# Attention's head tiles in three pools, a third item's scores among the query products

## The chip, the cores and the metric

One core of a Trainium2 chip runs the whole kernel. The metric is device time in microseconds (us); several executions of a kernel agree within about 0.3%.

## What is computed

One transformer layer over 1024 latent tokens (a grid of 16 rows and 64 columns) and 256 context tokens, width 1024, all in fp32: a half-step SwiGLU, then two token mixers side by side on one normalised input, merged by sigmoid gates and one output projection, then a second half-step SwiGLU. The mixers are neighbourhood attention (NA) and multi-head latent attention (MLA), 8 heads each. NA, cut to what matters:

```python
rs = jnp.clip(r - kh // 2, 0, n_rows - kh)
...
bias = rpb[:, row_off[None, None, :, None], col_off[:, :, None, :]]
s_loc = jnp.einsum('bjqhd,bjakhd->bhjqak', q_r, k_b).astype(jnp.float32) + bias.astype(jnp.float32)
s_loc = jnp.where(valid[:, :, None, :], s_loc, neg).reshape(B, H, n_blk, NA_QCOLS, n_loc)
s_ctx = jnp.einsum('bjqhd,bkhd->bhjqk', q_r, k_ctx).astype(jnp.float32)
p = jax.nn.softmax(jnp.concatenate([s_loc, s_ctx], axis=-1), axis=-1).astype(v.dtype)
...
o = (jnp.einsum('bhjqak,bjakhd->bjqhd', p_loc, v_b)
     + jnp.einsum('bhjqk,bkhd->bjqhd', p[..., n_loc:], v_ctx))
```

Each latent query attends to an 8 by 16 window of the grid, with a bias by head and offset, and to all 256 context keys. MLA attends to all 1280 tokens, with keys of 64 plain and 32 rotated dimensions.

## The kernel before

Every fp32 matrix product is made of three fp32r products of high and low halves. The first SwiGLU, the projections and the second SwiGLU run from plans: lists of steps for TensorE, with side steps (loads, splits, evictions) spread over them by position (`plan.step`, `plan.spread`). The last main steps before attention are `q_heads(1)`, numbered from `o`: four rotary steps, then four products whose results are stored to scratch memory. Stores are held back some steps and written behind the last step at the latest (`store`, `flush`).

Attention follows as a loop over 64 items: 8 NA heads of 4 items (blocks of columns j, 256 queries each), then 8 MLA heads of 4. Its parts:

- An item's `scores()` makes its context and local scores in two halves (s = 0, 1); VectorE adds the bias while it evicts the local scores (L1983), copies the context scores (L1954), and ScalarE takes the exponential (L1992).
- Its `values()` has three parts for NA: `local`, `context`, `edge`. Each transposes a piece of the probabilities and returns a product with the values, which is written `LAG` = 2 parts later. So the context and edge products of item n are written inside item n + 1.
- In the loop, item n's parts are interleaved with the scores of item n + `AHEAD` (3). The first `EARLY` items' scores are made already beside the products of `q_heads(1)`, into tiles of the pool "f" (`first_scores`, `first_soft`). With EARLY = 2, item 0 of the loop makes the scores of items 2 and 3.
- `NaHead.loads` fetches a head in steps. The first fetches q, ql (high and low query), kvc (context keys, and later context values), k and the first bias table: eight transfers of 256 or 64 KB in the order q, ql, kvc, q, ql, kvc, k, k, and one bias table. The others fetch bias table 2, values va (items 0 and 1 of the head) and vb (items 2 and 3), bias table 3. For head h of 2 and more the first step is written at item 4h - 4, behind its second part (`ahead_head`), the rest at item 4h - 3, just before the first scores of head h. Item 0 of a head uses bias table 1, items 1 and 2 table 2, item 3 table 3.
- All these tiles come from the pool "w" of 13 tiles of 4 KB per partition, but for the third bias table, which comes from "y" (2 tiles). `MlaHead` takes six tiles of "w", `FirstMerge` one at a time.

A tile is given out again when its last reader in the program is through; the load into it waits for that reader. TensorE's instructions and all transfers (issued by SP, one queue) keep the order in which the program writes them; so SP runs ahead of the other engines up to the first transfer whose tile is not free, and everything behind that transfer stands. VectorE, ScalarE and GpSimd have their order in attention from the compiler's scheduler.

Of the kernel before, what the change touches and what calls it, by code (L numbers as in the profile page):

```python
# [8 lines left out]
F32 = mybir.dt.float32  # L9
F32R = mybir.dt.float32r  # L10
# [5 lines left out]
P = 128  # L16
# [22 lines left out]
def f32(ap):  # L39
    return ap.bitcast(F32)  # L40
# [3 lines left out]
def hybrid_block(ctx: ExitStack, tc: tile.TileContext, a: dict, out: bass.AP):  # L44
# [9 lines left out]
    pools = {}  # L54

    def nm(s):
        count[0] += 1
        return f"{s}_{count[0]}"

    def open_pool(key, name, bufs, side):  # L60
        pools[key] = tc.alloc_tile_pool(name=nm(name), bufs=bufs, side=side, reuse_waits="tile")

    def close_pools(*keys):
        for key in keys:
            pools.pop(key).release()

    def U(dt=F32, key="u"):
        return pools[key].tile([P, 1024], dt, tag="u", name=nm("x" + key))
# [1 line left out]
    def V(dt=F32):  # L70
        return U(dt, "v")

    def W(dt=F32R):
        return pools["w"].tile([P, 1024], dt, tag="w", name=nm("w"))

    def T2(dt=F32, n=512):
        return pools["t"].tile([P, n], dt, tag="t", name=nm("t"))
# [34 lines left out]
    class Engine:  # L112


        def __init__(self, e):
            self.e = e
# [5 lines left out]
    def ld(dst, src):  # L122
        for x in [x for x in waiting if x[1].tensor.name == src.tensor.name]:
            waiting.remove(x)
            put(*x[1:])
        return put(dst, src)
# [4 lines left out]
    def put(dst, src):  # L131
        return pin(nc.sync.dma_start(dst, src))
# [987 lines left out]
    class Raw:  # L1120

        us = {(name, hl): [U(F32R, "v") for _ in range(2)] for name in ("a11", "a12") for hl in range(2)}
        f = {}
# [95 lines left out]
    plan = Plan()  # L1219
# [23 lines left out]
    o = len(plan.main)  # L1243
# [64 lines left out]
    o = len(plan.main)  # L1308
# [12 lines left out]
    o, tail = down1.plan(plan)  # L1321
# [110 lines left out]
    def emit_lat(d, ci, x, bank):  # L1432
        t, sq = T2() if bank else x, T2()

        def high():
            if bank:
                act.copy(t, x)
            store(cqT[d][:, ci * 512:(ci + 1) * 512], t)
            act.activation(sq, t, AF.Square)
            later(add, 1)  # L1440

        def add():
            if ci in squares:
                vec.tensor_tensor(squares[ci], squares[ci], sq, op=ALU.add)
            else:
                squares[ci] = sq
        later(high)

    for p in range(3):
        punits.append(Unit(h2, [wc_cols(2 * p), wc_cols(2 * p + 1)],  # L1450
                           lambda i, ci, x, bank, p=p: emit_lat(2 * p + i, ci, x, bank)))
# [21 lines left out]
    o = len(plan.main)  # L1473
# [67 lines left out]
    class Set:  # L1541
# [16 lines left out]
        def loads(self):  # L1558

            return [lambda j=j: self.load(j) for j in range(2)]  # L1560
# [50 lines left out]
    o = len(plan.main)  # L1611
# [97 lines left out]
    class NaHead:  # L1709


        def loads(self, h):
            self.h = h
            i, b = h // 2, (h % 2) * 64
            self.q, self.ql, self.kvc, self.k = q, ql, kvc, k = [W() for _ in range(4)]
            for s in range(2):
                o = 64 * s
                ld(f32(q[o:o + 64, :]), qas[i][0, b:b + 64, :])
                ld(f32(ql[o:o + 64, :]), qas[i][1, b:b + 64, :])
                ld(f32(kvc[o:o + 64, 0:256]), kas[i][s, b:b + 64, NLAT:])  # L1720
            for s in range(2):
                ld(f32(k[64 * s:64 * s + 64, :]), kas[i][s, b:b + 64, :NLAT])
            self.bias = [W(F32)]
            ld(self.bias[0][:, :768], a["bias"][h, 0])
            yield
            self.bias.append(W(F32))
            ld(self.bias[1][:, :768], a["bias"][h, 1])
            self.va = va = W()
            for j in range(2):
                self.values(va, j)  # L1730
            yield
            ld(f32(kvc[:, 256:512]), vcs[h])
            self.vb = vb = W()
            for j in range(2, 4):
                self.values(vb, j)
            yield
            self.bias.append(U(F32, "y"))
            ld(self.bias[2][:, :768], a["bias"][h, 2])
            yield

        def values(self, v, j):
# [3 lines left out]
    def na_loads(h):  # L1745
        heads["na", h] = x = NaHead()
        yield from x.loads(h)
# [97 lines left out]
    o = va_at  # L1845
# [9 lines left out]
    o = len(plan.main)  # L1855
# [4 lines left out]
    o = len(plan.main)  # L1860
# [3 lines left out]
    o = len(plan.main)  # L1864
# [3 lines left out]
    o = len(plan.main)  # L1868
    plan.step(*calls(q_heads(1, cqn[1]), 9))
    heads = {}  # L1870
    EARLY, AHEAD = 2, 3

    na_open = {}

    def na_next(h, n=1):
        if h not in na_open:
            na_open[h] = na_loads(h)
        for _ in range(n):
            next(na_open[h], None)

    def weights():
        close_pools("v")
        open_pool("w", "weights", 13, "left")
        open_pool("f", "first", EARLY, "left")

    def score_banks():
        banks[0] = "mv"
# [3 lines left out]
    def first_scores(j):  # L1891
        if len(early) == j:
            it = na_item(0, j)
            started.append(it)
            early.append(it.scores())
        next(early[j], None)
# [3 lines left out]
            soft.pop(0)()  # L1900

    plan.spread([weights], o - 4, o - 3)
    plan.spread([lambda h=h: na_next(h) for h in (0, 0, 0, 1)], o - 3, o + 5)
    plan.spread([score_banks], o + 2, o + 3)
    plan.spread([lambda j=j: first_scores(j) for j in (0, 0, 1, 1)], o + 4, o + 8)
    plan.spread([first_soft] * 2, o + 6, o + 9)

    ona, omla = [], []

# [138 lines left out]
    class MlaHead:  # L2048
        def __init__(self, h):
            self.h = h  # L2050
            self.qh, self.ql, self.kh, self.kl, self.v, self.kvc = [W() for _ in range(6)]
            b, i = (h % 2) * 64, (h % 4) * 32
            for s, x in enumerate((self.qh, self.ql)):
                ld(f32(x[0:64, :]), qns[h // 2][s, b:b + 64, :])
                ld(f32(x[64:QK, :]), qrs[h // 4][s, i:i + 32, :])
                ld(f32(self.kvc[0:64, s * 256:(s + 1) * 256]), kns[h // 2][s, b:b + 64, NLAT:])
                ld(f32(self.kvc[64:QK, s * 256:(s + 1) * 256]), krs[s, :, NLAT:])
            for s, x in enumerate((self.kh, self.kl)):
                ld(f32(x[0:64, :]), kns[h // 2][s, b:b + 64, :NLAT])
                ld(f32(x[64:QK, :]), krs[s, :, :NLAT])  # L2060
            vsv = vs[:, h * P:(h + 1) * P].rearrange("(t p) c -> p t c", p=P)
            ld(f32(self.v).rearrange("p (t c) -> p t c", t=8), vsv[:, 0:8, :])
            ld(f32(self.kvc[:, 512:768]).rearrange("p (t c) -> p t c", t=2), vsv[:, 8:10, :])
# [70 lines left out]
    soft, started = [], []  # L2134
    edges = []
    def na_item(h, j):
        if (j == 0) if h else (j == EARLY):
            na_next(h, 4)
        return NaItem(heads["na", h], j)

# [5 lines left out]
    def items_():  # L2146
        for h in range(NH):
            for j in range(4):
                yield lambda h=h, j=j: na_item(h, j)
        for h in range(NH):  # L2150
            for b in range(4):
                yield lambda h=h, b=b: mla_item(h, b)
# [6 lines left out]

    close_pools("u", "t")  # L2160
    open_pool("o", "heads", 16, "right")
    open_pool("y", "third", 2, "right")
    open_pool("t", "half", 12, "right")
    open_pool("u", "units", 10, "right")
    for x in (ona, omla):
# [9 lines left out]
    def ahead_head(h):  # L2175
        if h < NH:
            na_next(h) if h > 1 else None
        else:
            heads["mla", h - NH] = MlaHead(h - NH)

    def start(n):

        if n < len(todo):
            it = todo[n]()
            started.append(it)
            yield from it.scores()
# [28 lines left out]
    for n in range(len(todo)):  # L2215
        ahead = chain(*[start(x) for x in (range(EARLY, AHEAD + 1) if n == 0 else (n + AHEAD,))])
        for d in range(2):
            if n == len(todo) - 6 + d:
                fm.load(d)
            if n == len(todo) - 5 + d:  # L2220
                fm.split(d)
        parts = started[n].values()
        soft_n, soft[:] = list(soft), []
        for x, part in enumerate(parts):
            pending.append(part())
            for _ in range(-(-len(soft_n) // (len(parts) - x))):
                soft_n.pop(0)()
            for _ in range(5 // len(parts)):
                next(ahead, None)
            if n % 4 == 0 and x == 2 and n // 4 + 1 < 2 * NH:  # L2230
                ahead_head(n // 4 + 1)
            if n >= len(todo) - 3 and (n, x) != (len(todo) - 3, 0) and len(fm.todo) > 4:
                fm.step()
            if len(pending) > LAG:
                pending.pop(0)()
        for _ in ahead:
            pass
    for w in pending:
        w()
        fm.step()  # L2240
# [1 line left out]
        fm.step()  # L2242
    pinned[0] = False

    close_pools("u", "t", "y", "f", "w")
    open_pool("t", "half", TBUFS, "left")
    open_pool("u", "units", 24, "left")

# [35 lines left out]
    plan = Plan()  # L2284
# [5 lines left out]
    for d in range(KD):  # L2290
        o = len(plan.main)
# [21 lines left out]
    plan = Plan()  # L2313
# [30 lines left out]
    o = len(plan.main)  # L2344
# [13 lines left out]
    o = len(plan.main)  # L2358
# [14 lines left out]
    o, tail = down2.plan(plan)  # L2373
# [108 lines left out]
```

## Time and profile before

| | us |
|---|---|
| median of 3 runs (2557.51 to 2558.33) | 2557.65 |
| profiled execution | 2555.57 |
| its span, first to last instruction | 2553.8 |
| TensorE busy in it | 2526.1 |
| VectorE busy | 1897.7 |
| ScalarE busy | 1249.9 |

The mean granted clock of TensorE is 0.999. The last query products run from 1304.7 to 1333 us of the span, NA from there to about 1457 and MLA to about 1750. In the rows that follow, PE is TensorE, PEld its weight loads, DVE VectorE, ACT ScalarE, POOL GpSimd, SP the engine that issues transfers; "SPq" is its instruction queue. `bs`, `bm`, `bv` are PSUM banks by their tag, `xf` and `xu` score tiles, `w` and `xy` tiles of the pools "w" and "y", `d` scratch memory, `t` half tiles. A timeline row gives start, length, engine, line, operation, what it writes and reads, shape, how many were merged into it, and in brackets the idle time before it with what ended it. A row of waits gives total, number and longest wait.

### The profile page before, as it was taken

Reading aid. Unit: us, or ns where it says so; the run is one execution under the profiler, and the core shown is the slowest. Engines: PE = TensorE matmul, PEld = TensorE weight load, DVE = VectorE, ACT = ScalarE, POOL = GpSimd, SP = SyncE. Lnnn points to the kernel's source line nnn. Section 1 sums busy time; section 2 is a strip of 40 time slices with the busy share of each in tenths; the row PEclk is TensorE's granted clock in tenths of the full one; section 3 lists DMA queues with packets and bytes.
Section 4 is the critical chain, followed back from the end, with each engine's and each line's share of the span. In section 5 each row is a group of like instructions: output and inputs, shape, how many; then the busy total and the mean of one; then the engine's idle time right before and its main releaser. Section 6 shows DMA issues by size and latency. Waiting matters only on the chain.

```text
span 2553.8 us, 38179 instructions
## 1 busy us (share of the span) xinstructions
PE 2526.1 (99%) x13007; PEld 2145.5 (84%) x13007; DVE 1897.7 (74%) x3627; ACT 1249.9 (49%) x2389; POOL 242.5 (9%) x425
## 2 busy tenths in 40 slices
PE   8999999999999999999999999999999999999998
PEld 6888888888888788889889999988888888888887
DVE  5788887898567687874559988886445888777557
ACT  6623223555346753333439888782355322233633
POOL 1000000000002100001007622220030000000001
PEclk9999999999999999999999999999999999999999
DMA  8477765779576665766899832215135667556755
GB/s 315 162 242 236 242 225 189 274 246 297 180 239 221 241 220 190 229 225 200 286 287 243 224 78 77 77 32 210 67 131 179 212 222 236 183 185 251 248 203 193
DMA packets 275475, 523.32 MB, mean 205 GB/s; under 512 B 33424, under 2 KB 84432, under 8 KB 275280
## 3 DMA queue, kind: packets, MB, share of 16 engines
q1 hardware_dynamic: 275280, 520.88, 61.6%
q8 instruction: 103, 1.69, 0.3%
q14 instruction: 92, 0.75, 0.1%
HBM read 375.47 MB, written 145.29 MB: 204 GB/s over the span
## 4 chain that ended last, share of the span: by engine, by line
PE 86%; ACT 6%; DVE 5%; issue 2%; POOL 0%; DMA 0%; DVEq 0%; POOLq 0%; ACTq 0%
PE bs L161 33%; PE bm L161 30%; PE bv L161 20%; ACT xu L2091 2%; PE bm L164 2%; DVE xu L1954 1%; PE bs L164 1%; ACT t L2117 1%; DVE t L2118 1%; DVE xv L120 1%; ACT xu L1992 1%; ACT t L2091 0%; ACT t L1926 0%; ACT t L120 0%; PE bv L164 0%
## 5 line engine op out<-in xcount | busy, mean ns | idle before, releaser
L120 ACT CAST xu<-t 128x512 fp32r<-128x512 f32 x589 | 346.8, 621 | 673.3 <-DVE t L120 558.1
L161 PE MATMUL bm<-xu,xu 128*128 128x512 f32 (+1 forms) x2442 | 596.0, 388 | 0.9 <-ACT t L120 0.9
L161 PEld LDWEIGHTS bm<-xu,xu 128*128 128x128 f32 x2442 | 450.1, 188 | 92.1 <-ACT t L120 2.0
L120 DVE TENSOR_TENSOR xu<-t,xu 128x512 fp32r<-128x512 f32 x589 | 383.0, 688 | 77.5 <-ACT xu L120 77.1
L161 PE MATMUL bs<-xu,xu 128*128 128x512 f32 (+2 forms) x1581 | 388.3, 384 | 0.0
L161 PE MATMUL bs<-xv,xu 128*128 128x512 f32 x1512 | 363.5, 389 | 0.2 <-DVE t L120 0.2
L161 PEld LDWEIGHTS bs<-xu,xu 128*128 128x128 f32 x1581 | 291.7, 188 | 58.0
L161 PE MATMUL bv<-xv,xu 128*128 128x512 f32 x1342 | 336.0, 389 | 0.0
L161 PEld LDWEIGHTS bs<-xv,xu 128*128 128x128 f32 x1512 | 283.5, 188 | 59.7 <-issue 1.0
L161 PEld LDWEIGHTS bv<-xv,xu 128*128 128x128 f32 x1342 | 251.6, 188 | 52.1
L120 DVE TENSOR_TENSOR xu<-xu,xu 128x512 fp32r<-128x512 f32 x282 | 190.0, 689 | 64.4 <-ACT xu L120 63.4
L120 DVE TENSOR_TENSOR t<-t,t 128x512 f32<-128x512 f32 (+4 forms) x350 | 221.2, 635 | 13.5 <-ACT t L120 8.8
L161 PE MATMUL bs<-w,w 96*128 96x512 f32 (+3 forms) x832 | 206.0, 365 | 5.4 <-DVE st L1983 5.4
L161 PE MATMUL bv<-xu,xu 128*128 128x512 f32 x722 | 191.5, 389 | 0.0
L120 POOL TENSOR_SCALAR st<-st 128x1 f32<-128x1 f32 x60 | 27.1, 452 | 1630.9 <-ACT t L120 1283.6
L120 ACT CAST xu<-xu 128x512 fp32r<-128x512 f32 x282 | 169.5, 621 | 11.3 <-DMA xu<-in_f1w 8.0
L161 PEld LDWEIGHTS bv<-xu,xu 128*128 128x128 f32 x722 | 135.5, 188 | 28.1
L161 PE MATMUL bm<-t,xu 128*128 128x256 f32 (+1 forms) x920 | 156.9, 332 | 0.0
L161 PEld LDWEIGHTS bm<-t,xu 128*128 128x128 f32 x920 | 137.4, 189 | 18.6
L161 PE MATMUL bv<-t,w 128*128 128x256 f32 x896 | 150.7, 288 | 1.9 <-DVE t L2118 1.4
L161 PEld LDWEIGHTS bv<-t,w 128*128 128x128 f32 x896 | 133.1, 190 | 17.5 <-DVE t L2118 6.0
L161 PEld LDWEIGHTS bs<-w,w 96*128 96x128 f32 (+1 forms) x832 | 123.2, 190 | 14.2 <-DVE st L1983 7.7
(231 smaller groups left out, 3192.6 us busy)
## 6 DMA issues: line engine op xcount, KB each, us to landing
d<-t SPq DMA_DIRECT2D x432, 256.0 KB, 2.9
t<-d SPq DMA_DIRECT2D x348, 256.0 KB, 5.0
xu<-in_f1w SPq DMA_DIRECT2D x104, 512.0 KB, 4.4
xu<-in_f2w SPq DMA_DIRECT2D x58, 512.0 KB, 4.7
t<-in_wada SPq DMA_DIRECT2D x112, 256.0 KB, 4.5
w<-d SPq DMA_DIRECT2D x112, 256.0 KB, 5.0
t<-in_f1w SPq DMA_DIRECT2D x77, 256.0 KB, 5.0
t<-in_f2w SPq DMA_DIRECT2D x77, 256.0 KB, 5.2
```

The source lines that it names most:

```text
L120: return lambda *x, **y: pin(f(*x, **y))
L161: return pin(nc.tensor.matmul(o, s, m, start=start, stop=stop, skip_group_check=open_group[0]))
L164: return pin(nc.tensor.transpose(o, x, i))
L1954: nc.vector.tensor_scalar(dst, src, 1.0, FMIN, op0=ALU.mult, op1=ALU.max, accum_out=m)
L1992: soft.append(lambda s=s: nc.scalar.activation(pr[s][:, :640], pr[s][:, :640], AF.Exp, bias=n_[:, s:s + 1], accum_out=l[:, s:s + 1]))
L2091: nc.scalar.activation(x, x, AF.Exp, bias=n_[:, s:s + 1], accum_out=l[:, i:i + 1])
L2117: nc.scalar.copy(t[0], pb)
L2118: nc.vector.tensor_tensor(t[1], pb, f32(t[0]), op=ALU.subtract)
```

## The change

The tiles of a head come from pools of their own kind. "w" has 8 tiles instead of 13 and holds q, ql, va, vb of every NA head, and kvc and k of the even ones; "p" (2 tiles, opened where attention opens its pools) holds kvc and k of the odd heads; "y" (4 tiles of 3 KB) all bias tables. For MLA, "w" holds query and key tiles; kvc comes from "x" (3 tiles, opened in the place of "f" when item 2 is through), the values from "p" (head 0's from "x"). EARLY is 3: three items' scores are made beside the query products, for which all four load steps of head 0 are spread there; the first step of head 1, which stood there, is now written behind the products and their stores, where attention opens its pools.

```diff
-    def W(dt=F32R):
-        return pools["w"].tile([P, 1024], dt, tag="w", name=nm("w"))
+    def W(dt=F32R, key="w", n=1024):
+        return pools[key].tile([P, n], dt, tag=key, name=nm(key))
...
-            self.q, self.ql, self.kvc, self.k = q, ql, kvc, k = [W() for _ in range(4)]
+            self.q, self.ql = q, ql = W(), W()
+            self.kvc, self.k = kvc, k = [W(key="p" if h % 2 else "w") for _ in range(2)]
...
-            self.bias = [W(F32)]
-            ld(self.bias[0][:, :768], a["bias"][h, 0])
-            yield
-            self.bias.append(W(F32))
-            ld(self.bias[1][:, :768], a["bias"][h, 1])
+            self.bias = []
+            for j in range(2):
+                self.bias.append(W(F32, "y", 768))
+                ld(self.bias[j], a["bias"][h, j])
+                if j == 0:
+                    yield
...
-            self.bias.append(U(F32, "y"))
-            ld(self.bias[2][:, :768], a["bias"][h, 2])
+            self.bias.append(W(F32, "y", 768))
+            ld(self.bias[2], a["bias"][h, 2])
...
-    EARLY, AHEAD = 2, 3
+    EARLY, AHEAD = 3, 3
...
-        open_pool("w", "weights", 13, "left")
-        open_pool("f", "first", EARLY, "left")
+        open_pool("w", "weights", 8, "left")
+        open_pool("y", "third", 4, "left")
+        open_pool("f", "first", 3, "left")
...
-    plan.spread([lambda h=h: na_next(h) for h in (0, 0, 0, 1)], o - 3, o + 5)
-    plan.spread([score_banks], o + 2, o + 3)
-    plan.spread([lambda j=j: first_scores(j) for j in (0, 0, 1, 1)], o + 4, o + 8)
-    plan.spread([first_soft] * 2, o + 6, o + 9)
+    plan.spread([lambda: na_next(0)] * 4, o - 3, o + 5)
+    plan.spread([score_banks], o + 1, o + 2)
+    plan.spread([lambda j=j: first_scores(j) for j in (0, 0, 1, 1, 2, 2)], o + 2, o + 8)
+    plan.spread([first_soft] * 3, o + 4, o + 9)
...
-            self.qh, self.ql, self.kh, self.kl, self.v, self.kvc = [W() for _ in range(6)]
+            self.qh, self.ql, self.kh, self.kl = [W() for _ in range(4)]
+            self.kvc = W(key="x")
...
+            self.v = W(key="p" if h else "x")
...
-        if (j == 0) if h else (j == EARLY):
+        if h and j == 0:
             na_next(h, 4)
...
-    open_pool("y", "third", 2, "right")
+    open_pool("p", "parts", 2, "right")
+    na_next(1)
...
+        if n == EARLY - 1:
+            close_pools("f")
+            open_pool("x", "parts", 3, "left")
```

More of the change, by code (lines that the diff above doesn't have):

```diff
@@ L2243, in hybrid_block @@
     pinned[0] = False
-    close_pools("u", "t", "y", "f", "w")
+    close_pools("u", "t", "p", "x", "y", "w")
     open_pool("t", "half", TBUFS, "left")
```

## The prediction

> **What bounds the kernel now.** I read the page first, then the stretch around the edited code by windows, then who TensorE and the DMA queue wait for there.
>
> ```profile
> PE 2526.1 (99%) x13007; PEld 2145.5 (84%) x13007; DVE 1897.7 (74%) x3627; ACT 1249.9 (49%) x2389; POOL 242.5 (9%) x425
> ```
>
> TensorE is busy 2526.1 of 2553.8 us, so a change that moves work about can win at most the 27.7 us between. What it can lose has no such limit: each idle microsecond of TensorE is added to the end. The edit touches the last query products and the neighbourhood (NA) attention:
>
> ```profile
> 1283.00:1317.00 34.00, 34.00 (x207) 30.34 (x206) 18.29 (x56) 7.44 (x14) 0.00 (x0) 1.00 1.01 309
> 1317.00:1333.00 16.00, 16.00 (x81) 13.59 (x80) 7.94 (x20) 5.90 (x10) 0.90 (x2) 1.00 0.83 245
> ```
> ```profile
> 1333.00:1343.00 10.00, 6.73 (x42) 5.35 (x41) 8.19 (x31) 6.01 (x14) 2.50 (x8) 1.00 0.78 251
> 1343.00:1460.00 117.00, 114.83 (x905) 112.17 (x904) 109.48 (x376) 108.62 (x261) 84.80 (x161) 1.00 0.91 243
> ```
>
> Columns: stretch, its length, busy time of PE, PEld, DVE, ACT, POOL, clock, DMA share, GB/s. The query products keep TensorE full with VectorE half free. The first 10 us of attention have a hole of 3.27 us. After it TensorE is full again, and the DMA engines are 91% busy: the heads' loads arrive hardly faster than they are used. TensorE's waits, from 1280 to 1460 and then from 1365 to 1460, and its two long ones:
>
> ```profile
> PE bs L161 <- DVE st L1983: 5.4, 7, 1.9
> ```
> ```profile
> PE bs L161 <- DVE st L1983: 2.1, 5, 0.7
> ```
> ```profile
> 1337.42 1.11 PE L161 MATMUL bs<-w,w 128*128 128x256 f32 x4 [1.39 <-DVE st L1983]
> ...
> 1341.92 1.10 PE L161 MATMUL bs<-w,w 128*128 128x256 f32 x4 [1.88 <-DVE st L1983]
> ```
>
> 1.39 + 1.88 = 3.27 us come from making items 2 and 3's scores at once while VectorE still drains the queries; 2.1 us in five small waits come later. That is all the change can take away here: 5.4 us, 0.21%.
>
> The DMA queue is what the edit really rearranges:
>
> ```profile
> 1289.46 5.42 SPq L132 DMA_DIRECT2D w<-d  x8
> ```
> ```profile
> 1307.42 8.99 SPq L132 DMA_DIRECT2D w<-d  x11
> ```
> ```profile
> 1335.23 0.41 SPq L132 DMA_DIRECT2D xy<-in_bias  x1
> ...
> 1340.83 9.26 SPq L132 DMA_DIRECT2D w<-d  x8
> ```
> ```profile
> 1353.00 2.45 SPq L132 DMA_DIRECT2D w<-in_bias  x2
> ...
> 1358.71 6.63 SPq L132 DMA_DIRECT2D w<-d  x8
> ```
>
> SP issues in program order and runs ahead of TensorE until a tile is not yet free. Each group "w<-d x8" is one head's q, ql, kvc, k (q, ql, kvc halves first, k last; 1.66 MB). Head 0's goes out at 1289, head 1's at 1309 (the last 8 of 11), head 2's from 1341, head 3's from 1359. A head's first scores stand one item after the place where its loads are written: head 2's (item 8) start at 1357.49 (below), 16.6 us after its first load. This lead is what 13 "w" tiles buy.
>
> **The change part by part.** *Third item made early.* Item 2's scores, 8 matmuls, move into the query products: two more groups like
>
> ```profile
> 1332.64 0.59 PE bs L161 x4
> ```
>
> (chain of waits), so these end 2 x 0.59 = 1.2 us later and attention does 1.2 us less: zero on TensorE. VectorE has 8 of 16 us free there and ScalarE 10 of 16; without this cover the item would cost what it costs in attention. The score banks switch a step earlier, head 0's third bias table comes earlier, the tables are 3 KB instead of 4 KB, and the merge's tiles come from smaller pools: nothing waits for these, 0 (bound: the 3.27 us hole stays).
>
> *Head 1's first loads move* from 1309 (beside the products) to behind all stores of the products. SP reaches that point where it now issues the first attention load, 1335.23, plus 1.2 = 1336.4. What eight such loads take is read from head 0's (time from issue to landing of the first, of the last, and of one with an idle queue, narrow windows of the DMA view):
>
> ```profile
> w<-d SPq DMA_DIRECT2D x1, 256.0 KB, 4.3
> ```
> ```profile
> w<-d SPq DMA_DIRECT2D x1, 256.0 KB, 6.1
> ```
> ```profile
> w<-d SPq DMA_DIRECT2D x1, 256.0 KB, 3.6
> ```
>
> First issue 1289.46 + 4.3 = 1293.8; the last is issued 0.6 before the group's end, 1294.3, + 6.1 = 1300.4. So the seven behind the first (1408 KB) take 6.6 us, 4.7 ns per KB; an undisturbed first lands in 3.6. Head 1 is complete at 1336.4 + 3.6 + 6.6 = 1346.6. Item 4's scores, which need it, start at 1341.92 now; the hole of 3.27 us is replaced by one of over 8: **+4.7 us** (from -3.3 if the loads were hidden to +6).
>
> *Thirteen tiles become eight, with two in "p" for odd heads.* Two heads' q, ql, kvc, k, va, vb need 12 tiles; now there are 10 (bias has its own 4; before, the 13 held two bias tables of a head, 11 for the rest, and the short-lived bias tiles were passed on). Who still holds a tile when head h is to load (items 4h-4 to 4h-3)? Even h: head h-1 holds q, ql, va, vb, head h-2 holds kvc and vb until item 4h-5's last products, which are issued inside item 4h-4. So q and ql load early, kvc waits for the context product, k for the edge product. Odd h: head h-1 holds all six, head h-2's vb the seventh; only q loads early, and ql, second in SP's order, waits for the edge product with everything behind it. How close that is to the first scores, one item from before:
>
> ```profile
> 1354.45 0.64 PE L161 MATMUL bv<-t,w 128*128 128x256 f32 x4
> 1354.93 0.60 PE L164 MATMUL bm<-ident,xu 128*128 128x128 f32 x4
> ...
> 1355.96 0.64 PE L161 MATMUL bv<-xu,w 128*128 128x256 f32 x4
> 1356.44 0.38 PE L164 MATMUL bm<-ident,xu 128*128 128x128 f32 x2
> ...
> 1357.49 0.84 PE L161 MATMUL bs<-w,w 128*128 128x256 f32 x4
> ```
>
> The context product ends at 1354.93, the edge product at 1356.44, the next head's scores begin at 1357.49: 2.56 and 1.05 us. How soon SP follows a release no row shows by itself; I take 0.2 us (0 to 0.5, which moves the sum by 2). Odd head: 0.2 + 3.6 + 1152 KB x 4.7 ns = 9.2 us, less 1.05 = 8.15 us idle. Even head, from kvc: 0.2 + 3.6 + 1088 KB x 4.7 ns = 8.9, less 2.56 = 6.35. TensorE takes its work in order, so nothing fills this, and as it was the bound, nothing gives it back. Heads 3, 5, 7 and 2, 4, 6: 3 x 8.15 + 3 x 6.35 = **+43.5 us**. Behind the blocked load stand k, both bias tables, va, vb; the bias lands last, VectorE may hold a score bank up to 0.6 us longer (0 taken), va and vb are used 11 us later and are hidden. The five small waits (late bias tables) drown in this: **-2.1**. Head 0 of the latent attention loads its last key tile behind the same edge product; its first use is some 2.7 us later, 0.2 + 0.6 + 3.6 - 2.7: **+1.9** (0 to 4). Its later heads are loaded four long items ahead: 0. Sum so far 4.7 + 43.5 - 2.1 + 1.9 = 48.0.
>
> *The clock.* TensorE would now be idle over 6 us seven times. What idleness does is seen at the two ends of the kernel:
>
> ```profile
> 8.86 0.87 PE L164 MATMUL bs<-ident,xv 128*128 128x128 f32 x3 [8.86 <-DVE st L120]
> ...
> 12.19 1.54 PE L161 MATMUL bv<-xv,sc 128*32 128x128 f32 x32
> ...
> 14.25 1.08 PE L161 MATMUL bv<-xv,sc 128*32 128x128 f32 x32
> ```
> ```profile
> 2538.55 6.96 PE L161 MATMUL bv<-xu,xu 128*128 128x512 f32 x30
> ```
> ```profile
> 2548.00:2549.00 1.00, 0.00 (x0) 0.00 (x0) 0.57 (x1) 0.00 (x0) 0.92 (x2) 1.00 0.78 311
> 2549.00:2550.00 1.00, 0.00 (x0) 0.00 (x0) 0.71 (x2) 0.00 (x0) 0.26 (x1) 0.65 0.59 234
> 2550.00:2553.80 3.80, 0.00 (x0) 0.00 (x0) 0.70 (x2) 0.00 (x0) 0.00 (x0) 0.50 0.37 138
> ```
>
> The last matmul ends at 2545.5; the granted clock falls to 0.50 in the slice from 2549, near 3.8 us after. The first matmuls run slow, and full speed comes between 12.19 and 14.25, about 4.3 us after 8.86. So an idle of 6 to 8 us should leave 4.3 us at half clock, 2.15 us lost: 7 x 2.15 = **+15 us** (0 to 15). [...]
>
> Sum: 48.0 + 15 = 63 us. The profiled execution took 2555.57 (span 2553.8), 2.1 below the median of the runs; 2557.65 + 63 gives 2620.7, and I forecast 2620 us, 2.4% slower. [...]
>
> **The rivals.** [...] *The bursts are faster*: the eight loads were measured between stores. At the 309 GB/s of the stretch 1283 to 1317 an odd head takes 0.2 + 3.6 + 3.8 - 1.05 = 6.55, an even one 4.85, head 1 costs 2.8: 34.2 + 2.8 + 1.9 - 2.1 = 37 us without the clock, 2594; with it 2609. *Heavier*: the blocked bias also holds VectorE and the second half of a half-speed stretch meets the next: 0.6 per head and another 10 us of slow clock, 2635. *Faster, the other side*: the loads are in time. This takes tiles released a full item earlier than I count: it decides where a head's last load is issued 9 us ahead of its first scores, and not 1 to 3. Then only the holes go: 2557.65 - 3.3 = 2554.4, or 2552.3 with the small waits. For it speaks only that DMA has 9% free; against it, that even with 13 tiles head 2's eight loads took SP 9.26 us from 1340.83, where head 0's took 5.42: they already wait for tiles.
>
> **How the numbers follow.** Full forecast 0.47, clock holds 0.26, faster bursts 0.13, heavier 0.06, loads in time 0.08. The likeliest's own range is 2608 to 2632; the range 2588 to 2636 takes in the clock and the bursts and leaves out the other side. About 0.2%, 5.1 us, is what a measurement here can tell from no change: loads in time divides 0.03 faster and 0.05 within; all else is slower, 0.92.
>
> **What would show it.** In the changed kernel: no wait of 1.4 and 1.9 us at the start but one of about 8 at item 4's scores; then an idle of 6 to 8 us before each head's first scores, in turn shorter and longer, ended by a DMA into "w" or "p"; SP waiting there for the edge product; the granted clock near 0.5 for some 4 us behind each; some 190 us of NA attention instead of 127 (175 where the clock holds). If SP issues a head's k more than 8 us ahead of its scores, my count of tiles is wrong and with it the forecast.

## The result, and the profile after

The changed kernel takes **2612.79 us** (median of 5, 2610.81 to 2614.78), the kernel before 2557.85 beside it (5 runs, 2557.51 to 2559.79): ratio 1.0214 [1.0203, 1.0225], 55 us slower. The forecast was 2620 in 2588 to 2636. The profiled execution of the changed kernel took 2614.47 (span 2612.7), 58.9 us more span than the one of before: it lies 1.7 above its median and that of before lay 2.1 below its own.

The engine row of the page, and TensorE's waits from 1330 to 1530 us (total, times, longest):

```profile
PE 2542.9 (97%) x13007; PEld 2161.2 (83%) x13007; DVE 1899.0 (73%) x3627; ACT 1247.6 (48%) x2389; POOL 242.4 (9%) x425
```
```profile
PE bs L161 <- DMA p<-d: 27.9, 8, 5.9
PE bs L161 <- DMA w<-d: 17.0, 7, 3.7
```

The same 13007 matmuls take 2542.9 - 2526.1 = 16.8 us longer, and TensorE is idle 2612.7 - 2542.9 = 69.8 us instead of 27.7, so 42.1 more: the two make the 58.9. In this stretch every wait is one of scores for a load into "p" or "w", 44.9 us, and the 5.4 us of waits for VectorE are gone: 39.5 of the 42.1 us. Windows of the start and of the NA attention (columns as before):

```profile
1333.00:1343.00 10.00, 6.97 (x42) 5.79 (x40) 6.91 (x23) 4.78 (x10) 1.53 (x6) 1.00 0.87 255
1343.00:1513.00 170.00, 128.92 (x883) 125.61 (x883) 108.01 (x368) 106.92 (x257) 82.25 (x155) 0.85 0.60 173
```

The latent heads' 512-column scores begin at 1511.76 instead of 1455.58, the DMA share has dropped from 0.91 to 0.60, and the mean granted clock is 0.85. On average nothing is saturated any more. The timeline of TensorE for heads 1, 2 and 3 (start, length, work, idle before it and what ended that) shows why:

```profile
1345.91 0.77 PE L161 MATMUL bs<-p,w 128*128 128x256 f32 x2 [5.94 <-DMA p<-d]
1348.08 0.98 PE L161 MATMUL bs<-p,w 128*128 128x384 f32 x2 [1.40 <-DMA p<-d]
...
1369.51 0.48 PE L161 MATMUL bs<-w,w 128*128 128x256 f32 x2 [3.67 <-DMA w<-d]
1371.61 0.98 PE L161 MATMUL bs<-w,w 128*128 128x384 f32 x2 [1.62 <-DMA w<-d]
...
1387.75 0.64 PE L161 MATMUL bv<-xu,w 128*128 128x256 f32 x4
...
1388.92 0.60 PE L164 MATMUL bm<-ident,xu 128*128 128x128 f32 x4
1394.56 0.76 PE L161 MATMUL bs<-p,w 128*128 128x256 f32 x2 [5.04 <-DMA p<-d]
1396.80 0.98 PE L161 MATMUL bs<-p,w 128*128 128x384 f32 x2 [1.48 <-DMA p<-d]
```

Each head stops twice: 256 columns are the context scores, which need q, ql and kvc, and 384 columns the local scores, which need k, last in the queue. The other side of the same wait is the DMA queue's timeline for heads 2 and 3, and what SP waited for from 1330 to 1520:

```profile
1363.22 3.64 SPq L132 DMA_DIRECT2D w<-d  x6
...
1380.77 7.45 SPq L132 DMA_DIRECT2D w<-d  x2
1388.27 0.59 SPq L132 DMA_DIRECT2D p<-d  x1
1388.91 1.23 SPq L132 DMA_DIRECT2D w<-d  x2
1390.18 1.87 SPq L132 DMA_DIRECT2D p<-d  x3
```
```profile
SPq L132 <- PE bm L164: 73.4, 15, 8.5
SPq L132 <- PE bs L161: 20.5, 5, 6.6
```

Head 3's q goes out at 1380.77. Its ql, the second of that group, goes out only as the group ends, 7 us later, and kvc and k leave by 1392.05. Twenty waits, 93.9 us together, hold SP behind TensorE's own work, and TensorE then waits for SP. The lead of 16.6 us of the kernel before has become one of 8 to 9 us, counted from the load that is held up, and TensorE sits out 5 to 7 of them. The clock, by windows of 3.41 us around head 3 (the low stretches of this trace, 6.83 and 10.24 us, and the 17.07 us at full speed between them are two, three and five times that):

```profile
1387.60:1391.01 3.41, 1.92 (x16) 1.68 (x14) 3.29 (x13) 2.89 (x9) 2.18 (x5) 1.00 0.53 125
1391.01:1394.43 3.42, 0.00 (x0) 0.00 (x0) 0.86 (x2) 1.58 (x4) 2.90 (x6) 1.00 1.08 240
1394.43:1397.84 3.41, 1.81 (x6) 1.57 (x7) 0.03 (x1) 0.00 (x0) 0.00 (x0) 0.50 1.00 289
1397.84:1401.25 3.41, 3.41 (x17) 3.41 (x17) 1.84 (x6) 0.59 (x1) 0.00 (x0) 0.50 1.06 385
```

The clock falls at the end of a window without matmuls, stays at 0.50 through one in which TensorE worked 1.81 of 3.41 us, and returns at the end of a full one. The clock falls at every head from 1 to 7, at the others after windows with 0 to 14% of matmuls: once for 10.24 us and six times for 6.83, 51.2 us at half speed.

### The profile page after: what moved, and what is told of

Its sections match the earlier page's. It is cut to its first block, busy times and chain, and to the rows that moved or that the text cites. A ratio compares the mean times of both kernels' runs of the same rounds, so it can differ in the third digit from the quotient of the medians.

```text
span 2612.7 us, 38179 instructions
## 1 busy us (share of the span) xinstructions
PE 2542.9 (97%) x13007; PEld 2161.2 (83%) x13007; DVE 1899.0 (73%) x3627; ACT 1247.6 (48%) x2389; POOL 242.4 (9%) x425
## 4 chain that ended last, share of the span: by engine, by line
PE 85%; ACT 4%; DMA 4%; DVE 3%; issue 2%; SPq 1%; POOL 0%; DVEq 0%; POOLq 0%; ACTq 0%
PE bs L161 33%; PE bm L161 28%; PE bv L161 21%; PE bm L164 2%; ACT xu L2096 2%; PE bs L164 1%; DVE xu L1957 1%; ACT t L2122 1%; DMA p<-d 1%; DVE t L2123 1%; DMA w<-d 1%; SPq L132 1%; DVE xv L120 1%; DMA xu<-in_f1w 1%; ACT t L120 0%
## 5 line engine op out<-in xcount | busy, mean ns | idle before, releaser
L161 PE MATMUL bs<-w,w 96*128 96x512 f32 (+2 forms) x512 | 150.2, 405 | 18.3 <-DMA w<-d 18.3
L2123 DVE TENSOR_TENSOR t<-bm,t 128x512 fp32r<-128x512 f32 x160 | 109.6, 687 | 29.6 <-ACT t L2122 29.1
L164 PE MATMUL bm<-ident,xu 128*128 128x128 f32 x826 | 129.7, 277 | 0.0
L1957 DVE TENSOR_SCALAR_CACHE_REDUCE xu<-bs 128x512 f32<-128x512 f32 (+1 forms) x186 | 110.2, 600 | 12.9 <-PE bs L161 12.6
```

The source lines that it names most:

```text
L161: return pin(nc.tensor.matmul(o, s, m, start=start, stop=stop, skip_group_check=open_group[0]))
L164: return pin(nc.tensor.transpose(o, x, i))
L1957: nc.vector.tensor_scalar(dst, src, 1.0, FMIN, op0=ALU.mult, op1=ALU.max, accum_out=m)
L2123: nc.vector.tensor_tensor(t[1], pb, f32(t[0]), op=ALU.subtract)
```

## The experiments

My theory: the tile count sets the whole loss. A head's loads wait for tiles of the head before, so each burst starts too late (some 43 us), and the clock falls behind each idle (some 12 to 17). Rivals: the loss is in the order of the loads or the pools' places rather than their number; or one late start at head 1 carries on through the heads; or the clock term is an appearance, and the time would be the same without it.

**Tiles alone, for the even heads.** Even heads from 2 on take kvc and k from "x", which stands empty during the NA attention, and "p" has a third tile:

```
- k = [W(key="p" if h % 2 else "w") ...]
+ k = [W(key="p" if h % 2 else "x" if h else "w") ...]
...
- open_pool("p", "parts", 2, "right")
+ open_pool("p", "parts", 3, "right")
```

> The changed kernel, but kvc and k of the even heads from 2 on come from "x" (3 tiles that stand empty during NA) and "p" has 3 tiles instead of 2: 14 tiles for two heads' 12, so every first load of heads 2 to 7 finds a free tile. If the shortage of tiles makes the idle times, all six pairs of them (5.0 to 7.2 us each) and their half-clock stretches vanish, and only head 1's late load stays (about +4 us and some 3 us of slow clock): 2563 us. If the loads themselves are too slow for the items (DMA rate), the idle times stay at 5 to 7 us: 2605 to 2615 us.

Measured: 2564.94 us (2563.73 to 2566.98), 1.003 [1.0018, 1.0042] of before. TensorE's waits from 1330 to 1530 in this kernel:

```profile
PE bs L161 <- DMA p<-d: 6.8, 2, 5.4
PE bs L161 <- DVE st L1986: 2.1, 3, 0.7
PE bs L161 <- DVE t L2018: 1.5, 1, 1.5
PE bs L161 <- DMA w<-d: 1.4, 2, 0.7
```

The long waits of heads 2 to 7, odd and even, are gone, with the order of the loads untouched; only head 1's (5.4 + 1.4, both in the first row) is left, and with it one low-clock stretch of 6.83 us (mean granted clock 0.98 from 1343 to 1513). Because head 1 is as late as in the changed kernel and nothing follows from it, the carry-on rival falls. What the even heads take from "x" also leaves "w" to the odd ones: 48 of the 55 us are this shortage, its clock included. (How much of it the third "p" tile does was not separated.)

**One tile more.** Only `open_pool("w", "weights", 8, "left")` becomes 9.

> The changed kernel with one tile more in "w", 9 instead of 8. By my count of tiles q, ql and kvc of every head then load early, and only k (2 x 256 KB) waits, for the context product of the head two before: 0.2 + 0.6 + 3.6 + 1.2 - 2.56 = 3.0 us idle before each of heads 2 to 7 at most, alike for odd and even, too short for the clock to fall: 2557.7 + 7 (head 1) + 6 x 2.5 to 3 = 2578 to 2583 us. If the DMA rate were the limit: unchanged, near 2613. If the order of slots is chosen otherwise than I count, odd and even heads still differ.

Measured: 2576.2 us (2575.76 to 2578.15), 1.0075 [1.0059, 1.0092], a little below the expected range. TensorE's waits from 1330 to 1530, and three windows of it:

```profile
PE bs L161 <- DMA p<-d: 11.5, 4, 5.1
PE bs L161 <- DMA w<-d: 6.3, 3, 2.5
PE bs L161 <- DVE t L2018: 2.4, 1, 2.4
```
```profile
1379.25:1382.67 3.42, 1.27 (x10) 1.09 (x10) 2.73 (x10) 2.90 (x8) 2.22 (x5) 1.00 1.00 299
1362.19:1365.60 3.41, 1.57 (x13) 1.58 (x13) 1.36 (x6) 2.19 (x5) 2.69 (x5) 1.00 0.95 268
1382.67:1386.08 3.41, 3.41 (x18) 3.41 (x17) 2.40 (x9) 0.71 (x4) 1.60 (x4) 0.50 1.05 385
```

One tile takes away 36.6 of the 55 us. Heads 2 to 7 now wait 1.84 to 2.83 us each, once and not twice, odd and even alike: only k is late. The loss is steep in the tiles because each tile that is free early moves a whole stretch of the in-order queue forward. The windows show something else: an idle of 2.15 us halved the clock where its window had 1.27 us of matmuls (37%), and one of 1.84 did not where its window had 1.57 (46%). Of the six idles, those of 2.15, 2.44 and 2.83 us brought the clock down, so the 3.0 us that I expected to be too short for it would not have been; one of 2.48 us did not, as a window's end divided it and the window below still had 1.96 us of matmuls (57%):

```profile
1437.28:1440.69 3.41, 1.96 (x15) 1.99 (x16) 1.06 (x4) 1.58 (x5) 2.49 (x6) 1.00 0.99 332
```

**The changed kernel with TensorE kept busy.** Before the first scores of heads 1 to 7, 40 (even) or 48 (odd) identity transposes into the context bank, whose results are overwritten:

```
+ if hd.h and j == 0:
+     for _ in range(48 if hd.h % 2 else 40):
+         turn_(cx[:, :P], ident, ident)
```

> The changed kernel with 40 (even heads) or 48 (odd) transposes of the identity put before the first scores of heads 1 to 7, into the bank that these scores then overwrite: 4.4 and 5.3 us of TensorE work that fits into its idle time and changes no load. If the idle costs twice, by the wait and by the half clock after it, the clock stays at full and the time falls by the 15 to 17 us of slow work: 2596 to 2599 us. If the half clock costs nothing beside the wait (hidden by the late loads that follow), the time stays at 2613, and longer if the transposes do not fit.

Measured: 2604.8 us (2602.72 to 2608.62), 1.0186 [1.0171, 1.0202]. It gains 8.0 us and misses its range, since the gap between context and local scores was left open: the clock still fell three times (mean 0.97 from 1343 to 1520), two of them after windows with 48 and 28% of matmuls:

```profile
1457.48:1460.89 3.41, 1.62 (x11) 1.49 (x12) 0.37 (x1) 0.00 (x0) 0.00 (x0) 1.00 1.03 347
1481.37:1484.78 3.41, 0.95 (x7) 0.54 (x5) 0.00 (x0) 0.00 (x0) 0.00 (x0) 1.00 1.02 245
```

**Busier still.** The same, with 12 more transposes between the context and the local scores of each of these heads:

```
+ if hd.h and j + s == 0:
+     for _ in range(12):
+         turn_(loc[:, :P], ident, ident)
```

> As e3_busy, with 12 more transposes of the identity (1.3 us) between the first context scores and the first local scores of heads 1 to 7, where the second part of the idle time lies. If the clock falls after a 3.41 us window in which TensorE is busy less than about half, as the windows of the runs so far show (falls at 0.00 to 0.48, none at 0.46 to 0.74), no window falls below that here, the clock never drops, and the 5 us that e3_busy still lost go: 2598 to 2601 us. If the drop is not what costs them: 2605 us as e3_busy, or more.

Measured: 2601.05 us (2599.47 to 2604.44), 1.0173 [1.0159, 1.0187], at the upper edge of what was expected. The windows from 1300 to 1600 of before, of the changed kernel and of this one:

```profile
1300.00:1600.00 300.00, 294.15 (x2128) 276.12 (x2127) 254.63 (x818) 236.96 (x545) 124.00 (x230) 1.00 0.62 171
```
```profile
1300.00:1600.00 300.00, 253.78 (x1715) 239.37 (x1714) 206.21 (x667) 190.21 (x439) 109.89 (x206) 0.91 0.54 155
```
```profile
1300.00:1600.00 300.00, 293.39 (x2212) 279.05 (x2211) 217.93 (x703) 201.99 (x467) 113.83 (x212) 1.00 0.58 163
```

TensorE looks as busy as before (293.39 against 294.15), the clock never falls (1.00 in these 300 us, 0.91 in the changed kernel's), and still the kernel is 43.2 us slower than the one before: the filling is work for nothing, and VectorE's 217.93, near the changed kernel's 206.21 and far from 254.63, shows that attention advances hardly faster. So the clock's share is 2612.79 - 2601.05 = 11.7 us by the medians, good to some us, since the runs of each kernel spread over 4 to 5 us, and more if the filling itself delays a score; the 16.8 us by which the matmuls of the two profiles differ are taken as its upper end. The appearance rival falls.

**Head 1 alone.** The kernel before, with only head 1's first loads moved behind the stores:

```
- plan.spread([lambda h=h: na_next(h) for h in (0, 0, 0, 1)], o - 3, o + 5)
+ plan.spread([lambda: na_next(0)] * 3, o - 3, o + 3)
...
+ na_next(1)
```

> The kernel before, with one part of the change alone: the first load step of head 1 is written behind the products' stores instead of beside the products; pools, EARLY and all else as before. My theory: item 4's scores wait for head 1's k until about 1346 (now 1341.9), and an idle time above 6 us drops the clock: +4 and +3, 2565 us, and no idle time at later heads. Rival: the loads are hidden behind the hole that is there already: 2558 us.

Measured: 2563.33 us (2562.9 to 2566.7), 1.0023 [1.0014, 1.0033]: +5.0 us. The first wait at the start, 1.39 us, stays; one of 6.72 has taken the place of the second, 1.88, and the clock fell once, for 6.83 us (mean 0.98 from 1343 to 1513):

```profile
1349.20 1.49 PE L161 MATMUL bs<-w,w 128*128 128x256 f32 x4 [6.72 <-DVE st L1983]
```
```profile
1348.58 0.56 DVE L1983 CUSTOM_DVE_ANT_0 xu<-bs,xy 128x384 f32<-128x384 f32 x1 [4.75 <-DMA xy<-in_bias]
```

The second row is VectorE's: it holds the score bank for head 0's last bias table ("xy"), which in this kernel stands in the queue behind head 1's moved loads. Head 1's k landed at 1346.64, 2 us before that table at 1348.56, so its own lateness would have made a hole of some 4 us (1342.48 to 1346.64) anyway; in the changed kernel, where the table goes out early, it is the loads that are waited for. 6.72 and 1.39, less the 3.27 of before, give 4.84 us more idle at the start. TensorE's matmuls also take 2528.8 - 2526.1 = 2.7 us longer in this profile, and the two profiles' spans differ by 8.9 us (2562.7 and 2553.8), the medians by 5.0 only: how the 5.0 divides between the wait and the clock is not settled.

**The third item alone.** The kernel before, with three items' scores made beside the queries (EARLY 3), and "w" 12 to make room:

```
- EARLY, AHEAD = 2, 3
+ EARLY, AHEAD = 3, 3
...
- open_pool("w", "weights", 13, "left")
+ open_pool("w", "weights", 12, "left")
```

and the spread of the first scores as in the changed kernel.

> The kernel before, with the third item alone: EARLY = 3, three score tiles in "f" and the scores spread over o + 2 to o + 7, for which "w" has 12 tiles instead of 13; head 1's loads, bias tables and pools as before. My theory: the two waits at the start of attention (1.4 and 1.9 us) go or halve, one tile less costs some tenths at the later heads: 2555 to 2557 us where before has 2558. Rival: the early scores are worth nothing, since VectorE's drain holds the next item all the same, and the missing tile costs 3 us idle per head: 2565 us or more.

Measured: 2562.65 us (2556.47 to 2563.01), 1.0013 [1.0005, 1.0022]. The expectation was wrong. The two holes of 1.39 and 1.88 us became one:

```profile
1343.46 1.49 PE L161 MATMUL bs<-w,w 128*128 128x256 f32 x4 [3.09 <-DVE st L1983]
```

Its window, 1339.42 to 1342.84, had 0.95 us of matmuls (28%) and the clock fell for 6.83 us. Here head 0's last bias table still goes out behind the stores, at 1338.65, and lands at 1342.81, just before the hole ends. Four of the 11 runs took 2556.5 to 2559.6 and seven 2562.0 to 2563.0; that the clock held in the short ones is not shown (the mean granted clock on record is 0.999 in the two shortest, 0.998 in the two others, and 0.997 to 0.999 in the long ones). Nor is the hole all that this kernel loses: with 12 tiles instead of 13, waits for loads that the kernel before does not have come back at the later heads:

```profile
PE bs L161 <- DMA w<-d: 2.9, 4, 1.1
```

**A version meant to beat both.** The changed kernel with "w" 10, the bias tables' pool 3, all six tiles of an odd head from "w", even heads' kvc and k from "x", and head 1's first loads back beside the query products:

```
- k = [W(key="p" if h % 2 else "w") ...]
+ k = [W(key="w" if h % 2 or h == 0 else "x") ...]
...
- open_pool("w", "weights", 8, "left")
+ open_pool("w", "weights", 10, "left")
- open_pool("y", "third", 4, "left")
+ open_pool("y", "third", 3, "left")
...
+ plan.spread([lambda: na_next(1)], o + 4, o + 5)
...
- na_next(1)
```

> The changed kernel with its space cut anew: "w" 10 tiles, "y" 3, so that head 1's first loads fit beside the query products again (o + 4); odd heads take all six tiles from "w", the even heads from 2 on take kvc and k from "x", "p" serves MLA's values only. 13 tiles and a pool of their own for the bias tables. If shortage and head 1's late load are the whole loss, nothing is idle before any head, the holes at the start are gone and the late bias tables too: 2552 to 2555 us, the fastest of all. If something else in the change costs time (the early third item, the smaller MLA pools), it shows here: 2558 us or more.

Measured: 2564.02 us (2561.41 to 2566.9), 1.0026 [1.0015, 1.0037]: 49 us better than the changed kernel, not better than the one before, and above the 2552 to 2555 us expected. Its waits from 1330 to 1530, and one later:

```profile
PE bs L161 <- DVE st L1987: 5.2, 5, 2.6
PE bs L161 <- DMA w<-d: 2.6, 2, 1.5
```
```profile
1753.98 2.37 PE L161 MATMUL bm<-xo,xu 128*128 128x512 f32 x5 [2.07 <-ACT xu L120]
```

No NA head waits for its loads; the 2.6 us of waits for "w" are those of the first two latent heads (1.10 at 1459.73, 1.50 at 1520.75). But a hole of 2.57 us stands at 1350.84, behind VectorE, as one of 3.09 did in the kernel with the third item alone and two of 3.27 us together in the kernel before. This fits a backlog of VectorE from the query products that still has to be worked off when the scores are early and the loads in time; which instructions must move to be rid of it was not tried. This hole and the one at 1753.98 also cost 3.41 us of low clock each. None of these kernels beats the one before, where at most 5.4 us were to be had.

## Why the prediction was right

**Direction and mechanism.** The predicted lead, eight "w" tiles against 13, decided it, and the two runs with more tiles confirm it. The other side, loads in time, fell: head 3's k left at 1391.45, 3.1 us ahead of its first scores and 5.35 ahead of its local ones, not 9. Measured against the four terms:

- *Odd heads*, 8.15 predicted: heads 3, 5, 7 wait 5.04 + 1.48 = 6.52, 6.90 and 7.18, mean 6.87. *Even heads*, 6.35 predicted: 5.29, 4.97, 5.14, mean 5.13. Together 36.0 instead of 43.5. This is the mis-sized term. The burst was right: from ql's issue at 1387.76 to k's landing at 1396.66 it takes 8.9 us, where the working had 9.0 without the 0.2 that I took for SP (no run shows that 0.2 by itself, only the burst as a whole). Two things made it too big. I treated the eight loads as needed at once, but the context scores run as soon as kvc is in, so 0.76 us of work (0.48 for even heads) splits the idle. And the count of who holds a tile was wrong for the odd heads: their ql does not wait for the edge product. It is issued at 1387.76, as that product starts (1387.75), and its wait is put down to scores, which fits head 2's last scores (made three items ahead) giving its query tiles back. So 1.76 us of work stood beside the burst until 1389.52 where the sum had 1.05 less 0.2. 8.9 + 0.14 until the scores start - 1.76 - 0.76 is the 6.52. For head 2 the same burst took 8.25 us, from kvc's issue at 1363.22 to k's landing at 1371.47, where the working had 8.7.
- *Head 1*: 5.94 + 1.40 = 7.34 us instead of "over 8"; less the 3.27 us of holes, which are gone, +4.1, predicted +4.7. The other edit at the start, the third item early, was put at zero and at most at the hole's staying. The kernel with it alone (and one tile less in "w") shows the second: the hole is not removed but moved.
- *Small waits*, -2.1: they are gone. *Latent head 0*, predicted +1.9: 1.62 us at 1513.86, and 1.26 more at 1574.65, where I had put later heads at 0.
- *Idle in all*: 36.0 + 4.1 - 2.1 + 2.9 = 40.9; the profile has 42.1, the rest lying upstream of the edit.
- *The clock*, predicted 15: between 11.7 and 16.8. Seven falls came as forecast, but not of 4.3 us: once 10.24 and six times 6.83. Each costs less than half its length, since TensorE is idle in part of it (head 3's has 5.22 us of matmuls in 6.83). That this term lies so near is in part luck: the low stretches were longer than forecast and cost less of their length.

Idle by 48.0 and clock by 15 gave 63; 43.2 and 11.7 were found by the medians, 42.1 and 16.8 in the profiles. The 8 us between 63 and 55 are mostly the bursts' overlap with TensorE's own work. Where I saw the heads' loads as hardly faster than their use, at a DMA share of 0.91, the share turned out to follow the tiles: 0.60 in the changed kernel, and 0.93 (from 1343 to 1460) in the kernel with tiles for the even heads, where no head from 2 on waits long. Inside a burst the DMA engines are full (1.08 in the window from 1391.01), ahead of it nearly idle (0.03 in the one from 1384.19).

## What to carry to other kernels

Count the live tiles at the place where the next block's loads are written: the queue, in order, stops at the first tile that isn't free (here twenty times, 93.9 us together), and what counts is how long before its first use the last load behind it can go out. Here the whole change cost 55 us with 8 tiles in "w" and 18 with 9; tiles borrowed for the even heads from a pool that stood empty, with one more for the odd ones, got 48 back, and most of what was left is head 1's later loads, not tiles. And add the clock to every repeated idle that can take up most of a 3.41 us window (in these runs it fell after windows with 0 to 39% of matmuls, and once with 48%): here it came to 27% (11.7 on 43.2 us) to 40% (16.8 on 42.1) on top of the idle.

## What the runs showed of the hardware

The clock did not need a window without work to fall: with nine tiles in "w" it fell after one with 1.27 us of matmuls in 3.42 (37%). In this case's runs it fell after 3.41 us windows with 0 to 39% of matmuls and once with 48% (the kernel with TensorE kept busy), and held after others with 46% (nine tiles) and more. In the changed kernel it came back after windows that were 97 to 100% busy, and windows of 21 to 69% left it low; one of 82% did so in the kernel with the third item alone. The 39% are from the version meant to beat both:

```profile
1751.08:1754.49 3.41, 1.34 (x6) 0.66 (x4) 1.23 (x2) 0.89 (x2) 0.00 (x0) 1.00 0.92 319
```

Low stretches were 3.41 us long in that version and 6.83 or 10.24 in the changed kernel, whole windows each. From head 2 on the falls of the changed kernel are 23.89 us apart, seven windows, while the heads' first scores are 22.9 to 25.6 us apart: the falls keep to the ends of windows, and that the loads lock to them is not shown. The share alone, as the profile models the ends of matmuls, does not settle when the clock falls, since 46% held in one run and 48% fell in another; what exactly the clock counts stays open. Transposes of the identity alone held it: in the busier kernel the window from 1362.49 to 1365.90 lies wholly within 40 of them, and the clock stayed at full.

```profile
1362.31 4.53 PE L164 MATMUL bs<-ident 128*128 128x128 f32 x40
```
```profile
1362.49:1365.90 3.41, 3.41 (x33) 3.41 (x32) 1.58 (x6) 2.32 (x5) 2.52 (x5) 1.00 1.04 232
```
